# Order of the token mixers inside a two-layer decoder trunk: which attention is projected and emitted ahead of the delta rule

## The chip, the cores and the metric

One core of one Trainium2 chip. TensorE (PE) multiplies, VectorE (DVE), ScalarE (ACT) and GpSimd (POOL) do elementwise work, SyncE (SP) issues most transfers. The metric is the device time of one execution in microseconds (us), as the median of several runs; lower is better. The numbers of a profile come from one execution that was recorded.

## What is computed

A trunk of two layers over one sequence of 512 tokens with 1024 features, in float32. Each layer is a feed-forward block, a mixer and a second feed-forward block, each followed by a layer norm:

```python
x = layer_norm(ALPHA * x + 0.5 * swiglu(x, ffn1_w_gu[l], ffn1_w_down[l]), ...)
mix = hybrid_mixer(x, w_in[l], ...)
x = layer_norm(ALPHA * x + mix, ...)
x = layer_norm(ALPHA * x + 0.5 * swiglu(x, ffn2_w_gu[l], ffn2_w_down[l]), ...)
```

The mixer projects `x` by `w_in` and runs three causal mixers side by side, whose outputs are concatenated and projected by `w_out`:

- softmax (differential) attention, 4 heads: the difference of two softmaxes of 32-wide queries and keys, on 64-wide values, then an RMS norm;
- stick-breaking attention, 4 heads of 64: each score passes a log-sigmoid, a reversed running sum along the keys and an exponential, then an RMS norm;
- the gated delta rule, 4 heads of 128: queries, keys and values pass a causal convolution of width 4 and Silu; in chunks a triangular system is solved; a scan over the chunks carries a 128x128 state per head; the output is normed and multiplied by Silu of a gate projection `z`.

## The kernel before, in words

Activations lie feature by token: 8 tiles of 128 features by 512 tokens. A float32 product is three passes over a rounded part and a rest (`mm3`, L99 to L105: weight high times x high, high times low, low times high). `Stream.get` (L73 to L95) loads a chunk of 8 weight blocks, rounds four blocks on ACT (L89) and takes the rest on DVE or, where `st.eng` is set, on POOL (L90). One projection tile (`full_tile`) is 8 blocks, so 24 matmuls of 512 columns, into a PSUM bank of the pool `pd` (two in the mixer).

The program is written in an emission order, and a planner turns it into one instruction order per engine: emission order is priority, and an instruction that is ready earlier may be put ahead. On the chip each engine runs its order as it stands.

`mixer` emits for a layer, before:

1. delta projections, the first four tiles in two halves beside the norm of the feed-forward block (`first_tiles`), then the others with their convolution (`convolved`, L503 to L519: one ACT and three DVE operations) and Silu; then the ACT table of exponentials is loaded (`preload`, L478);
2. `squares` (L521), beta and decay from L549 on;
3. `project_v` (L805), 96 matmuls for the values of both attentions;
4. `triangles` (L850): key products (L537), their norms, the triangles of each head (L611 to L636), then `base` (L640), the solve of 16x16 blocks on DVE in 15 serial steps (L652, L654), reached through DRAM by transfers on SP's queue;
5. the first pair of stick-breaking query and key tiles (`project_qk`, L822). Each is split into a rounded part and a rest, and slices of the two are stacked by SBUF-to-SBUF transfers on SP (L846);
6. stick-breaking attention of heads 0, 1 and of heads 2, 3 (`attend(1, 0)` with the second pair of tiles in its middle, `attend(1, 1)`). A unit is 128 queries of one head: scores (L878, L879), ACT and DVE operations (L931 to L939), transposes (L902), a copy (L904) and the product with the values (L907). `finish` and `turned` (L970) end a pair of heads;
7. two of the four gate tiles (`gate`, L984);
8. `delta` (L859): doubling of the solved blocks (L667 to L680), joins (L686 to L705), operands (L708 to L717), and `state`, the scan over four chunks (L720 to L751), with a norm at each second chunk and a turn (L776, L779);
9. the first pair of softmax query and key tiles, softmax attention of heads 0, 1 (with the second pair in its middle) and 2, 3, with row maxima at L915;
10. the other two gate tiles, Silu of the gates (`silus`, L472, which waits behind the last exponential), product with the delta output, residual sums on POOL (L134), and `split` (L992, L993) of the eight parts;
11. the output projection by `w_out`: `head` computes four tiles first over six parts and then over the last two, in the part order 2, 3 (stick-breaking), 4 to 7 (delta), 0, 1 (softmax).

The wide tiles of queries, keys, values, convolved tiles, gates and parts come from one pool (`wide`, `KQV` = 26 buffers). Delta's work tiles `inv` have 11 buffers. `psc` (two PSUM banks) holds scores, `po` and `pt` outputs and transposes of attention; `products` borrows all four for the four heads' key products until the triangles have read them.

Of the kernel before, what the change touches and what calls it, by code (L numbers as in the profile page):

```python
# [9 lines left out]
F32 = mybir.dt.float32  # L10
# [6 lines left out]
P = 128  # L17
# [17 lines left out]
KQV = 26  # L35
# [201 lines left out]
def ffn(g, idx, final, mixes):  # L237
    nc = g.nc
    st = g.st
    with g.tc.tile_pool(name="ffn", bufs=NJ, reuse_waits="tile") as fp, \  # L240
# [8 lines left out]
        def post(j, pg, pu):  # L249
# [6 lines left out]
            if j == 4:  # L256
                g.settled = i
            nc.vector.tensor_tensor(out=sg, in0=pu, in1=sg, op=ALU.mult)  # L258
# [167 lines left out]
def mixer(g, l):  # L426
# [14 lines left out]
    def pd():  # L441
        return g.pd.tile([P, T], F32, name="pd")
# [42 lines left out]
    b0 = st.take(12 * KD)  # L485
# [3 lines left out]
    heads_in = [pd(), py(), py(), pav.tile([P, T], F32, name="po")]  # L489
    first_tiles(g, [(b0 + i * KD, p) for i, p in enumerate(heads_in)])  # L490
# [12 lines left out]
    def convolved(h, b, pre=()):  # L503
        tiles = []
        for w, dst in enumerate((kT, qT, vT)):
            if w < len(pre):
                p = pre[w]
            else:
                p = pd()
                full_tile(g, b + w * KD, p)  # L510
# [8 lines left out]
        return silus(tiles)  # L519
# [22 lines left out]

    st.eng = nc.gpsimd
    st.queue = nc.scalar
    ends = []
    for h in range(HEADS):
        ends += convolved(h, b0 + 3 * h * KD, (heads_in[:3], heads_in[3:])[h] if h < 2 else ())
    preload(ends)
    for h in range(HEADS):  # L549
        squares(h)  # L550
# [61 lines left out]
    def triangle(h):  # L612
# [10 lines left out]
        LT = mp.tile([P, NC, P], F32, name="inv", bufs=11)  # L623
# [16 lines left out]
    def base(h0, n):  # L640
# [17 lines left out]
        for h in range(h0, h0 + n):  # L658
            XT[h] = mp.tile([P, NC, P], F32, name="XT", bufs=4)
            nc.sync.dma_start(out=XT[h], in_=slabs(g.scr[1], h))  # L660
            X[h] = mp.tile([P, NC, P], F32, name="inv", bufs=11)
            nc.sync.dma_start(out=X[h], in_=slabs(g.scr[2], h))


    def double(h):
# [5 lines left out]
        Y = mp.tile([P, NC, P], F32, name="inv", bufs=11)  # L671
# [12 lines left out]
    def join(h, m):  # L684
# [6 lines left out]
        Y = mp.tile([P, NC, P], F32, name="inv", bufs=11)  # L691
# [15 lines left out]
    def operands(h):  # L707
# [3 lines left out]
        kd[h] = mp.tile([P, NC, P], F32, name="inv", bufs=11)  # L711
# [4 lines left out]
        vb[h] = mp.tile([P, NC, P], F32, name="inv", bufs=11)  # L716
# [84 lines left out]


    V = []

    def project_v():  # L805
        bv = st.take(4 * KD)
        pv = [py(), py()] + [pav.tile([P, T], F32, name=n) for n in ("po", "pt")]
        for k in range(KD):
            xhi, xlo = g.x[k]
            hi, lo = st.get(bv + 4 * k, 4)  # L810
            for c in range(NC):
                nc.tensor.matmul(out=pv[c], lhsT=xhi[:, ch(c)], rhs=hi, start=k == 0, stop=False)
                nc.tensor.matmul(out=pv[c], lhsT=xhi[:, ch(c)], rhs=lo, start=False, stop=False)
                nc.tensor.matmul(out=pv[c], lhsT=xlo[:, ch(c)], rhs=hi, start=False, stop=k == KD - 1)
        for c in range(NC):
            y = wide()
            nc.scalar.copy(out=y, in_=pv[c])
            V.append(y)

    qb, kb_, qa, ka = [], [], [], []  # L820

    def project_qk(q, k, sc, b, w):  # L822

        n = P // w
        for dst, f in ((q, sc), (k, 1.0)):
            p = pd()
            full_tile(g, b, p)
            b += KD  # L830
            hi, lo = wide(F32R), wide(F32R)
            nc.scalar.mul(out=hi, in_=p, mul=f)
            nc.vector.scalar_tensor_tensor(out=lo, in0=p, scalar=f, in1=hi.bitcast(F32), op0=ALU.mult, op1=ALU.subtract)
            if dst is q:
                rows = [[hi, lo] * (n // 2)]
            elif n == 2:
                rows = [[hi, hi], [lo, lo]]
            else:
                rows = [[hi, hi, lo, lo]]
            for i in range(n):  # L840
                own = slice(w * i, w * i + w)
                ts = []
                for r in rows:
                    t = wide(F32R)
                    for j, src in enumerate(r):
                        nc.sync.dma_start(out=t[w * j:w * j + w].bitcast(F32), in_=src[own].bitcast(F32))  # L846
                    ts.append(t)
                dst.append(ts)
# [193 lines left out]
    def head():  # L1042

        tiles = [pd(), pd(), py(), py()]
        for a, b in ((0, 6), (6, KD)):
# [7 lines left out]
            if b < KD:  # L1053
                st.use([g.ws] * 3 + [g.wx] * 5)
                for i in range(3):
                    st.get(bo + 4 * KD + i * PC)
# [194 lines left out]
```

## Time and profile before

| what | us |
|---|---|
| median of 3 runs | 2254.13 |
| lowest, highest | 2253.29, 2255.03 |
| the profiled execution | 2255.08 |
| its span, first to last instruction | 2252.1 |
| PE busy | 2141.5 |
| DVE busy | 1153.2 |
| ACT busy | 886.4 |
| POOL busy | 346.7 |

Busy time is the time in which an engine has an instruction under way; pipelined matmuls overlap, so the time from one start to the next tells what a further one costs. A wait names the instruction that ended it, as far as the semaphores tell. PEclk is the granted clock of TensorE as a share of 2.4 GHz, as a mean over a stretch.

### The profile page before, as it was taken

How to read it: one execution, taken by the hardware profiler on the slowest of the kernel's cores; microseconds unless marked ns; L12 is line 12 of the kernel's file. 1: busy time of each engine (PE TensorE's matmuls, PEld its weight loads, DVE VectorE, ACT ScalarE, POOL GpSimd, SP SyncE). 2: the span in 40 equal slices, each digit the busy share in tenths (PEclk: the TensorE clock that was granted, in tenths of full speed). 3: DMA queues.
4: the chain of work that ended last, by engine and by line, in shares of the span. 5: the costliest groups of instructions: out<-in, count | busy, mean ns of one | idle time of the engine just before them, and what ended most of it. 6: DMA issues, size and time to landing. Idle time of an engine off the chain costs nothing.

```text
span 2252.1 us, 29920 instructions
## 1 busy us (share of the span) xinstructions
PE 2141.5 (95%) x11382; PEld 1792.2 (80%) x11382; DVE 1153.2 (51%) x2347; ACT 886.4 (39%) x1755; POOL 346.7 (15%) x295
## 2 busy tenths in 40 slices
PE   8999999997988999999999999999989889999997
PEld 7888889876767888888888888898768668888886
DVE  4533436455687843333563334274566788333426
ACT  4333324545554533332443333155454635333313
POOL 1100011442113500000130000024511144000010
PEclk9999999999998999999999999999999889999998
DMA  6433323335221233332333333233442213333322
GB/s 186 128 94 97 97 75 104 94 97 135 76 67 47 84 104 100 96 94 75 113 103 96 100 94 94 66 104 103 113 101 76 76 48 103 94 95 100 96 66 94
DMA packets 89742, 213.08 MB, mean 95 GB/s; under 512 B 21840, under 2 KB 36208, under 8 KB 89600
## 3 DMA queue, kind: packets, MB, share of 16 engines
q1 hardware_dynamic: 81696, 183.27, 26.8%
q10 hardware_dynamic: 6912, 25.17, 3.7%
q0 software_dynamic: 992, 2.75, 0.7%
q8 instruction: 89, 1.46, 0.3%
q14 instruction: 53, 0.43, 0.1%
HBM read 189.64 MB, written 6.83 MB: 87 GB/s over the span
## 4 chain that ended last, share of the span: by engine, by line
PE 79%; DVE 12%; DMA 3%; ACT 2%; issue 2%; SPq 1%; POOL 1%; ACTq 0%; POOLq 0%; DVEq 0%
PE pd L104 23%; PE pd L103 23%; PE pd L105 23%; DMA wraw<-in_w 2%; DVE wlo L90 2%; PE po L907 1%; DVE x L212 1%; ACT whi L89 1%; DVE lt L166 1%; DVE at L937 1%; DMA kqv<-kqv 1%; PE psc L878 1%; DVE x L220 1%; PE pt L902 1%; DVE x L163 1%
## 5 line engine op out<-in xcount | busy, mean ns | idle before, releaser
L89 ACT CAST whi<-wraw 128x512 fp32r<-128x512 f32 x692 | 423.1, 620 | 990.8 <-PE pd L104 798.6
L90 DVE TENSOR_TENSOR wlo<-wraw,whi 128x512 fp32r<-128x512 f32 x580 | 431.0, 750 | 640.3 <-ACT whi L89 628.1
L103 PE MATMUL pd<-x,whi 128*128 128x512 f32 (+1 forms) x1888 | 714.6, 379 | 6.6 <-ACT x L1169 6.1
L104 PE MATMUL pd<-x,whi 128*128 128x512 f32 (+1 forms) x1888 | 715.6, 379 | 1.7 <-POOL x L231 1.1
L105 PE MATMUL pd<-x,wlo 128*128 128x512 f32 (+1 forms) x1888 | 713.3, 378 | 3.1 <-DVE wlo L90 3.1
L103 PEld LDWEIGHTS pd<-x,whi 128*128 128x128 f32 x1888 | 357.1, 190 | 70.9 <-ACT x L1169 6.1
L105 PEld LDWEIGHTS pd<-x,wlo 128*128 128x128 f32 x1888 | 357.6, 189 | 66.4 <-DVE wlo L90 3.3
L104 PEld LDWEIGHTS pd<-x,whi 128*128 128x128 f32 x1888 | 357.6, 189 | 66.3 <-POOL x L231 3.0
L103 PE MATMUL pd<-hhi,whi 128*128 128x512 f32 (+1 forms) x880 | 307.7, 350 | 0.0
L104 PE MATMUL pd<-hlo,whi 128*128 128x512 f32 (+1 forms) x880 | 307.6, 350 | 0.0
L105 PE MATMUL pd<-hhi,wlo 128*128 128x512 f32 (+1 forms) x880 | 307.2, 349 | 0.0
L90 POOL TENSOR_TENSOR wlo<-wraw,whi 128x512 fp32r<-128x512 f32 x112 | 151.9, 1360 | 297.8 <-ACT whi L89 214.2
L168 POOL TENSOR_TENSOR lt<-lt 128x512 f32<-128x512 f32 x26 | 39.2, 1509 | 1016.2 <-ACT lt L165 1012.1
L103 PEld LDWEIGHTS pd<-hhi,whi 128*128 128x128 f32 x880 | 165.4, 188 | 24.4
L105 PEld LDWEIGHTS pd<-hhi,wlo 128*128 128x128 f32 x880 | 165.4, 188 | 24.2
L104 PEld LDWEIGHTS pd<-hlo,whi 128*128 128x128 f32 x880 | 165.4, 188 | 24.1
L258 DVE TENSOR_TENSOR lt<-pd,lt 128x512 f32<-128x512 f32 x88 | 60.4, 690 | 112.6 <-PE pd L105 111.2
L134 POOL TENSOR_TENSOR x<-x 128x512 f32<-128x512 f32 x48 | 74.1, 1581 | 74.1 <-DVE ams L957 70.6
L515 DVE SCALAR_TENSOR_TENSOR kqv<-pd,conv,kqv 128x511 f32<-128x511 f32 (+2 forms) x54 | 40.3, 747 | 60.4 <-ACT kqv L513 59.4
L260 DVE TENSOR_TENSOR hlo<-lt,hhi 128x512 fp32r<-128x512 f32 x88 | 67.1, 765 | 6.2
L231 POOL TENSOR_TENSOR x<-x 128x256 fp32r<-128x256 f32 x60 | 45.9, 766 | 152.1 <-ACT x L229 148.3
L165 ACT ACTIVATE lt<-x 128x256 f32<-128x256 f32 (+1 forms) x58 | 29.5, 512 | 100.0 <-DVE x L163 99.8
(307 smaller groups left out, 2300.0 us busy)
## 6 DMA issues: line engine op xcount, KB each, us to landing
wraw<-in_w SPq DMA_DIRECT2D x300, 512.0 KB, 3.5
wraw<-in_w ACTq DMA_DIRECT2D x48, 512.0 KB, 3.6
kqv<-kqv SPq DMA_DIRECT2D x128, 64.0 KB, 2.0
kqv<-kqv SPq DMA_DIRECT2D x48, 128.0 KB, 3.8
scr<-zero POOLq DMA_DIRECT2D x2, 1032.0 KB, 11.4
x<-in_xT SPq DMA_DIRECT2D x8, 256.0 KB, 5.9
scr<-inv SPq DMA_DIRECT2D x8, 256.0 KB, 3.4
XT<-scr SPq DMA_DIRECT2D x8, 256.0 KB, 5.2
```

What stands on the lines that cost most here:

```text
L89: nc.scalar.copy(out=hi, in_=r)
L90: (eng or self.eng or nc.vector).tensor_tensor(out=lo, in0=r, in1=hi.bitcast(F32), op=ALU.subtract)
L103: nc.tensor.matmul(out=out, lhsT=whi, rhs=xhi, start=first, stop=False)
L104: nc.tensor.matmul(out=out, lhsT=whi, rhs=xlo, start=False, stop=False)
L105: nc.tensor.matmul(out=out, lhsT=wlo, rhs=xhi, start=False, stop=last)
L134: i = g.nc.gpsimd.tensor_tensor(out=t, in0=xhi.bitcast(F32), in1=xlo.bitcast(F32), op=ALU.add)
L165: nc.scalar.activation(out=sq[:, r], in_=t[:, r], func=AF.Square)
L168: eng.tensor_tensor(out=self.acc2[:, r], in0=self.acc2[:, r], in1=sq[:, r], op=ALU.add)
L231: eng.tensor_tensor(out=xlo[:, r], in0=t[:, r], in1=xhi[:, r].bitcast(F32), op=ALU.subtract)
L258: nc.vector.tensor_tensor(out=sg, in0=pu, in1=sg, op=ALU.mult)
L260: nc.vector.tensor_tensor(out=hlo, in0=sg, in1=hhi.bitcast(F32), op=ALU.subtract)
L515: nc.vector.scalar_tensor_tensor(out=y[:, s:], in0=p[:, :T - s], scalar=wc[:, 3 - s:4 - s], in1=y[:, s:], op0=ALU.mult, op1=ALU.add)
```

## The change

The order of emission in the mixer is turned round, and the weights are packed in the new order. The new order is: stick-breaking queries and keys (now the four tiles of `first_tiles`, stacked at once by the new helper `stack`, behind a table load that waits for the last Silu of the feed-forward block), values, beta and decay, the whole of stick-breaking attention with its `flush`; then the twelve delta projections with convolutions, Silu and a second table load, squares; then the first softmax pair, `triangles` and `delta`; then softmax attention, all four gate tiles, and the end. The last turns of the scan are set aside and put behind softmax attention. The output projection takes parts in their own order, with four attention parts first, of which all splits are on POOL; `head` is halved at four parts. `KQV` is 27 and `inv` has 10 buffers.

```diff
-KQV = 26
+KQV = 27
+            g.lastsilu = i
+    def stack(p, dst, f, w, keys):
+        n = P // w
+        hi, lo = wide(F32R), wide(F32R)
+        nc.scalar.mul(out=hi, in_=p, mul=f)
+        nc.vector.scalar_tensor_tensor(out=lo, in0=p, scalar=f, in1=hi.bitcast(F32), op0=ALU.mult, op1=ALU.subtract)
...
+                    nc.sync.dma_start(out=t[w * j:w * j + w].bitcast(F32), in_=src[own].bitcast(F32))
...
+    bq = st.take(4 * KD)
+    heads_in = [pd(), pd(), py(), pav.tile([P, T], F32, name="po")]
+    first_tiles(g, [(bq + i * KD, p) for i, p in enumerate(heads_in)])
+    st.eng = nc.gpsimd
+    st.queue = nc.scalar
+    preload([g.lastsilu])
+    for i, p in enumerate(heads_in):
+        stack(p, (qb, kb_)[i % 2], (0.125, 1.0)[i % 2], 64, i % 2)
+    project_v()
...
-        LT = mp.tile([P, NC, P], F32, name="inv", bufs=11)
+        LT = mp.tile([P, NC, P], F32, name="inv", bufs=10)
...
-    project_v()
-    triangles()
-    bq = st.take(4 * KD)
-    project_qk(qb, kb_, 0.125, bq, 64)
-    attend(1, 0, lambda: project_qk(qb, kb_, 0.125, bq + 2 * KD, 64))
-    attend(1, 1)
-    gate(2)
-    delta()
+    attend(1, 0)
+    attend(1, 1)
+    flush()
+    b0 = st.take(12 * KD)
+    tiles = []
+    for h in range(HEADS):
+        tiles += convolved(h, b0 + 3 * h * KD)
+    preload(silus(tiles))
+    for h in range(HEADS):
+        squares(h)
     bp = st.take(4 * KD)
     project_qk(qa, ka, 32.0 ** -0.5, bp, 32)
+    triangles()
+    delta()
+    turns_left = later[:]
+    del later[:]
     attend(0, 0, lambda: project_qk(qa, ka, 32.0 ** -0.5, bp + 2 * KD, 32))
-    for o in oab[2:]:
+    attend(0, 1)
+    flush()
+    for f in turns_left:
+        f()
+    gate(HEADS)
+    silus(zs)
+    for o in oab:
         split(o, nc.gpsimd)
-    attend(0, 1)
-    while later:
-        later.pop(0)()
-    gate(HEADS - 2)
-    silus(zs)
...
-    st.use([g.wx] * WX, [g.ws] * 3)
+    st.use([g.ws] * WS, [g.wx] * 2)
...
-    for o in oc + oab[:2]:
+    for o in oc:
         split(o)
-    order = [2, 3, 4, 5, 6, 7, 0, 1]
+    order = list(range(KD))
...
-        for a, b in ((0, 6), (6, KD)):
+        for a, b in ((0, 4), (4, KD)):
```

## Rows read from the trace of the kernel before

**Rows 1.** The page, part 1: busy us, share of span, instructions.
```profile
PE 2141.5 (95%) x11382; PEld 1792.2 (80%) x11382; DVE 1153.2 (51%) x2347; ACT 886.4 (39%) x1755; POOL 346.7 (15%) x295
```
**Rows 2.** Windows of layer 1's mixer: length, busy by engine, PEclk, DMA share, GB/s.
```profile
380.00:454.00 74.00, 72.51 (x417) 62.31 (x416) 38.08 (x75) 39.95 (x73) 34.13 (x31) 1.00 0.26 79
454.00:481.00 27.00, 25.49 (x112) 20.21 (x111) 8.59 (x23) 11.04 (x24) 9.84 (x8) 0.94 0.26 78
481.00:544.00 63.00, 54.93 (x311) 44.40 (x309) 47.02 (x126) 33.43 (x81) 26.75 (x22) 1.00 0.50 126
544.00:580.00 36.00, 28.83 (x184) 24.45 (x184) 18.47 (x36) 19.63 (x45) 5.42 (x3) 0.91 0.29 74
580.00:601.00 21.00, 21.00 (x257) 14.72 (x257) 6.19 (x18) 9.75 (x29) 3.84 (x3) 1.00 0.45 119
...
608.00:641.00 33.00, 32.41 (x227) 28.23 (x227) 25.69 (x97) 14.52 (x37) 0.00 (x0) 1.00 0.20 51
641.00:656.00 15.00, 13.81 (x94) 11.49 (x93) 13.16 (x56) 12.00 (x41) 4.15 (x6) 1.00 0.29 72
656.00:706.00 50.00, 35.68 (x148) 27.22 (x149) 38.19 (x95) 27.24 (x69) 10.44 (x7) 0.73 0.21 64
```
**Rows 3.** Windows of layer 2's mixer, two of its stretches.
```profile
1598.00:1660.00 62.00, 54.42 (x308) 44.07 (x307) 46.65 (x126) 32.96 (x79) 27.30 (x22) 1.00 0.52 129
...
1773.00:1823.00 50.00, 36.26 (x151) 27.56 (x150) 37.77 (x95) 27.34 (x69) 9.66 (x7) 0.73 0.20 63
```
**Rows 4.** Waits of PE, 380 to 706: total us, times, longest.
```profile
PE psc L878 <- DMA kqv<-kqv: 7.6, 3, 3.8
PE pt L970 <- DVE at L964: 6.8, 2, 4.4
```
**Rows 5.** Timeline of PE, products: start, us, tiles and shape, count.
```profile
483.76 1.06 PE L537 MATMUL pt<-kqv 128*128 128x128 f32 x8
```
**Rows 6.** Timeline of PE from 640 to 707, with idle before and its releaser.
```profile
640.22 0.39 PE L750 MATMUL pa<-vn,intra 128*128 128x128 f32 x2
...
658.44 0.39 PE L103 MATMUL pd<-kqv,whi 128*128 128x512 f32 x1
658.66 0.39 PE L104 MATMUL pd<-kqv,whi 128*128 128x512 f32 x1
...
692.06 0.73 PE L103 MATMUL pd<-kqv,whi 128*128 128x512 f32 x2 [1.80 <-ACT kqv L992]
...
704.94 0.65 PE L970 MATMUL pt<-ident,at 128*128 128x128 f32 x4 [2.33 <-DVE at L964]
```
**Rows 7.** Groups of DVE, 380 to 641: count, busy us, mean ns, idle before.
```profile
L515 DVE SCALAR_TENSOR_TENSOR kqv<-pd,conv,kqv 128x511 f32<-128x511 f32 (+2 forms) x27 | 20.2, 747 | 30.2 <-ACT kqv L513 29.7
L937 DVE TENSOR_TENSOR_SCAN at<-at 128x384 f32<-128x384 f32 (+3 forms) x16 | 15.4, 960 | 0.3
L938 DVE TENSOR_TENSOR at<-psc,at 128x384 f32<-128x384 f32 (+3 forms) x16 | 7.8, 488 | 0.3
...
L654 DVE TENSOR_TENSOR blk<-blk,blkt 128x15 f32<-128x15 f32 (+7 forms) x15 | 5.1, 342 | 0.3
```
**Rows 8.** Timeline of ACT behind the scan and at the gates' Silu.
```profile
640.64 0.37 ACT L792 COPY o<-pa 128x256 f32<-128x256 f32 x1 [0.70 <-PE pa L750]
...
649.57 0.84 ACT L779 ACTIVATE x<-pa,dng 128x256 f32<-128x256 f32 x2
...
685.86 1.28 ACT L472 ACT_TABLE_LOAD   x1
687.15 0.63 ACT L472 ACTIVATE kqv<-kqv 128x512 f32<-128x512 f32 x1
```
**Rows 9.** Groups of PE, 507 to 585: the scores of stick-breaking attention.
```profile
L878 PE MATMUL psc<-kqv 128*128 128x384 f32 (+3 forms) x32 | 10.1, 383 | 10.1 <-DMA kqv<-kqv 7.2 <-DVE at L938 1.7 <-DVE blk L654 1.2
```
**Rows 10.** Timeline of SP's queue: issues of the stacking copies.
```profile
609.09 4.94 SPq L846 DMA_DIRECT2D kqv<-kqv  x8
```
**Rows 11.** Groups of PE, 603 to 706: first passes of the output projection.
```profile
L103 PE MATMUL pd<-kqv,whi 128*128 128x512 f32 x12 | 5.6, 478 | 1.8 <-ACT kqv L992 1.8
...
L103 PE MATMUL psc<-kqv,whi 128*128 128x512 f32 x7 | 3.1, 473 | 0.0
```

More of the change, by code (lines that the diff above doesn't have):

```diff
@@ L482, in preload, with project_v, project_qk @@
             g.after(table, i)
-    b0 = st.take(12 * KD)
+    V = []
+    qb, kb_, qa, ka = [], [], [], []
+    def project_v():
+        bv = st.take(4 * KD)
+        pv = [pd(), pd()] + [pav.tile([P, T], F32, name="pt"), py()]
+        for k in range(KD):
+            xhi, xlo = g.x[k]
+            hi, lo = st.get(bv + 4 * k, 4)
+            for c in range(NC):
+                nc.tensor.matmul(out=pv[c], lhsT=xhi[:, ch(c)], rhs=hi, start=k == 0, stop=False)
+                nc.tensor.matmul(out=pv[c], lhsT=xhi[:, ch(c)], rhs=lo, start=False, stop=False)
+                nc.tensor.matmul(out=pv[c], lhsT=xlo[:, ch(c)], rhs=hi, start=False, stop=k == KD - 1)
+        for c in range(NC):
+            y = wide()
+            nc.scalar.copy(out=y, in_=pv[c])
+            V.append(y)
+    def stack(p, dst, f, w, keys):
[3 more added lines that the diff above has]
+        nc.vector.scalar_tensor_tensor(out=lo, in0=p, scalar=f, in1=hi.bitcast(F32), op0=ALU.mult, op1=ALU.subtract)
+        if not keys:
+            rows = [[hi, lo] * (n // 2)]
+        elif n == 2:
+            rows = [[hi, hi], [lo, lo]]
+        else:
+            rows = [[hi, hi, lo, lo]]
+        for i in range(n):
+            own = slice(w * i, w * i + w)
+            ts = []
+            for r in rows:
+                t = wide(F32R)
+                for j, src in enumerate(r):
+                    nc.sync.dma_start(out=t[w * j:w * j + w].bitcast(F32), in_=src[own].bitcast(F32))
+                ts.append(t)
+            dst.append(ts)
+    def project_qk(q, k, sc, b, w):
+        for keys, dst, f in ((0, q, sc), (1, k, 1.0)):
+            p = pd()
+            full_tile(g, b, p)
+            b += KD
+            stack(p, dst, f, w, keys)
+    bq = st.take(4 * KD)
[7 more added lines that the diff above has]
+    project_v()
     kT, qT, vT = [], [], []
@@ L501, in mixer, with convolved @@
     nc.scalar.copy(out=ba, in_=p[0:2 * n])
-    def convolved(h, b, pre=()):
+    def convolved(h, b):
         tiles = []
         for w, dst in enumerate((kT, qT, vT)):
[L506 to L510, printed above, removed]
+            p = pd()
+            full_tile(g, b + w * KD, p)
             y = wide()
@@ L518, in convolved @@
             tiles.append(y)
-        return silus(tiles)
+        return tiles
     def squares(h):
@@ L541, in products @@
         nc.vector.tensor_scalar(out=xs[:, 0, h], in0=xs[:, 0, h], scalar1=RMS_EPS, scalar2=None, op0=ALU.add)
[L543 to L550, printed above, removed]
     gb = pa()
@@ L670, in double @@
             nc.tensor.matmul(out=pt[:, c], lhsT=lx[:, c], rhs=X[h][:, c], start=True, stop=True)
-        Y = mp.tile([P, NC, P], F32, name="inv", bufs=11)
+        Y = mp.tile([P, NC, P], F32, name="inv", bufs=10)
         nc.scalar.copy(out=Y, in_=pt)
@@ L800, in mixer @@
     nm = Norm(g, 3 * l + 1, ALPHA, LN_EPS)
[L803 to L848, printed above, removed]
     def triangles():
@@ L1053, in head @@
             if b < KD:
+                for d in range(4):
+                    st.get(bo + d * KD + PC)
                 st.use([g.ws] * 3 + [g.wx] * 5)
-                for i in range(3):
-                    st.get(bo + 4 * KD + i * PC)
     def ahead(*pools):
@@ L1207, in split_in @@
     v = np.concatenate([va, vb], axis=1).reshape(KD, P, 4, P).transpose(0, 2, 1, 3)
-    return sum(heads, []) + [v] + pairs(qb, kb) + [blocks(z)[:2]] + pairs(qa, ka) + [blocks(z)[2:]]
+    return pairs(qb, kb) + [v] + sum(heads, []) + pairs(qa, ka) + [blocks(z)]
 def kernel(**inputs):
```

13 lines of the change are left out of this document (7 added, 6 removed).

## The prediction

> **What bounds the kernel now.** I read the page first, then the mixer's two stretches by windows, then TensorE's waits, then single lines. PE is busy 95% of the span, so a reordering can win only where it is not [rows 1]. That is the mixer. Each layer's, from its first projection to the point where the output projection runs without a break, is the stretch from 380 to 706 (326 us) in layer 1 and from 1498 to 1823 (325 us) in layer 2; the two have the same shape [rows 2, 3]. Its stages, in layer 1: delta projections 380 to 454, value projection to 481, then the delta chain 481 to 641 (products and base solve to 544, doubling to 580, joins to 601, operands to 608, scan to 641), and a tail to 706. PE idles 8.1 us in the base-solve stretch, 7.2 in the doubling stretch and 14.3 in the last 50 us, where the granted clock is a mean 0.73 as well [rows 2]; layer 2's last stretch says the same, 13.7 and 0.73 [rows 3].
>
> Two waits make up much of that. Scores of the stick-breaking attention wait for copies of stacked queries and keys (7.6 us in three waits), and the transposes of finished attention blocks wait for VectorE (6.8 us) [rows 4]. The tail has a plain cause. The gates' Silu must come behind the softmax attention's last Exp: its table load stands at 685.86 and the first Silu at 687.15 [rows 8]; the output projection of a delta head waits for its split and starts at 692.06, and the softmax attention's last transposes come at 704.94, although the scan's last matmul starts at 640.22 [rows 6]. So 65 us pass behind the scan.
>
> **The change part by part.** The kernel's instructions are ordered by a planner: emission order is priority, and a ready instruction of lower priority fills a gap. I therefore add up, per layer, a front, the delta chain and a tail.
>
> *Front.* One projection tile is 24 matmuls. At 0.23 us each (starts 658.44 and 658.66 [rows 6]) that is 5.5 us. Before, 12 delta tiles and the value projection (96 matmuls, four tiles) stand ahead of the chain: 16 x 5.5 = 88.3 us. With 16 small beta/gate matmuls (3.7 us at the same pace) and 16 transposes of the squares (at 0.11 us each, from eight that end after 1.06 us, one alone taking some 0.27 [rows 5]; 1.8 us) that is 93.8; the stretch took 101 [rows 2], so 7.2 us were lost. After, four stick-breaking tiles come ahead too: 20 x 5.5 = 110.4, plus 5.5 as before, plus the whole of stick-breaking attention, which is emitted ahead of the delta projections. Its PE work: 40 transposes and 80 value matmuls at 0.11 us (13 us), 32 score matmuls (10.1 us as pipelined busy time for the bulk of them [rows 9], about 7 by starts) and the masks: 21 us, an estimate. The sum is 137; with the loss of before, and 4 us more for friction, 148. The friction is bounded: the DVE work in this stretch is 16 scans of 0.96 us and two elementwise operations of 0.49 us beside each (31 us in all), and 36 convolution steps of 0.75 us (27 us) [rows 7]; 58 us in some 85 us of PE work is not a bound, but a convolution tile holds one of two PSUM banks for an ACT operation and three such steps, behind attention's. Between nothing and 15 us I take 4, since the stretch from 380 to 454 ran the same convolutions at 98% PE busy. Then the first pair of softmax query/key tiles, emitted ahead of the products: 11 us. It hides the last convolution, its Silu and the table load (1.28 us [rows 8]; there are two more loads per layer, one hidden here, one behind the FFN's last Silu under the projections). The chain starts at 148 + 11 = 159 us instead of 101.
>
> *Chain.* Before it is 160 us [rows 2]. What shortens it: stick-breaking attention was emitted ahead of the doubling and so had priority in it; softmax attention is emitted behind the scan and fills only. Base stretch, 63 us: the 15 steps' larger operation needs 5.1 us of DVE [rows 7], but softmax units take DVE and ACT in the same place, and products to triangles is DVE work that stays; I take 59. The copies of stacked queries and keys pass the base solve's transfers on SP's queue: the first softmax pair has 32 of them, 20 us of issue at 8 in 4.94 us [rows 10], over before the gather some 28 us into the chain. Doubling, 36 us: 7.2 idle go with the score waits, of which the longest stands inside it, and stick-breaking's own 7 us or so of PE go; 22, between 36 and the 9 us that its 80 matmuls of 128 columns need. Joins, 21 us, filled with three large matmuls in every gap: 18. Operands, the 7 us from 601 to 608, stay. Scan, 33 us, filled with softmax units in both kernels, with fewer projections after: 28. The sum is 134. Ends: 160 if nothing gets shorter; 115 if the idle 15 us and a third of the foreign PE work go (PE is busy 144 of the 160 us, some 50 of it the chain's own by counts and 0.11 us).
>
> *What fills the chain.* Softmax attention (21 to 24 us of PE), its second projection pair (11) and four gate tiles (22) are PE work of 55 us beside some 50 of the chain's own in 134. Slots decide when: 27 wide tiles hold 12 convolved, 4 value and 8 softmax tiles, so the second pair cannot be stacked before the first two softmax heads are done (about 60 us into the chain at the 4 us per unit that the tail of before shows), and comes to its end at about 120. That is ahead of the scan's end.
>
> *Tail.* Behind the last scan step of before, copy, square, norm, transposes and scaling run from 640.64 to 650.4 [rows 8]; the product with the gate and the split add 3 us. The first half of the output projection (4 tiles x 4 parts x 3 matmuls, 11 us) needs only attention outputs and hides most of it. By 706, before had issued 19 groups of three of the output projection [rows 11], against 16 here: 9 matmuls, 2 us. The tail is 15 us instead of 65. The residual sums (POOL, eight) and the attention splits move to POOL ahead of it, under the scan and the gates; uncovered, the splits would cost 6 us. Smaller pools (10 instead of 11 delta buffers) cost nothing while two buffers stay free in the doubling.
>
> *Sum.* 159 + 134 + 15 = 308 against 326: 18 us per layer, 36 in both. The profiled execution took 2255.1 us (2252.1 span and 3.0 around it), 1 us above the median: 2255.1 - 36 - 1 = **2218**.
>
> **A rule that speaks against it.** In the last 50 us of before PE is busy 35.7 us and the granted clock is a mean 0.73, between full (2.4 GHz) and half (1.2 GHz) [rows 2]; the clock fell behind PE's gaps there. The Trainium skill, "TensorE: Matmul & The Clock Gate", section "HAM oscillation — how this bites in real kernels", says that a kernel whose PE keeps pausing is throttled again and restarts cold each time. By that rule the chain, now with 55 us of filler for 134 us, would itself run cold; the trace agrees for the old tail.
>
> **The rivals.** (1) *The chain is the bound and does not shrink.* It starts 58 us later, and if it takes 160 us the mixer is 159 + 160 + 15 = 334 us, 8 more per layer: 2270, slower. It decides from a chain of 152 us on. For it: the base stretch is latency of small DVE steps and DMA round trips, and its length is the same in both layers [rows 2, 3]. Against: the waits of [rows 4] in it.
> (2) *Cold clock.* The chain's matmuls of 128 columns, 264 by the code, take 0.11 us more each at half clock, 29 us, of which I put 12 on the path, the rest beside other work: 24 us in two layers, 2242. For it: 0.91 already in the doubling stretch [rows 2]. Against: the chain is mostly DVE, ACT and DMA latency.
> (3) *Softmax attention is late.* If its second half ends 17 us behind where I put it, because slots come late, the gates' Silu waits for it as before and the mixer takes 325 us: 2252, no change that can be told.
> (4) *The chain runs nearly alone*, 115 us: 289 per layer, 2181.
> (5) *Attention and delta projections do not overlap*: attention's units are a string of ACT and DVE operations, and if the planner leaves PE idle beside them, its 16 units take some 45 us (31 of DVE alone [rows 7]) where I counted 21: 24 us per layer, 2266.
>
> **How the numbers follow.** Forecast 0.45, (1) 0.13, (2) 0.15, (3) 0.10, (4) 0.12, (5) 0.05. A change under 0.2% (4.5 us) is about what a measurement here can tell from none. Faster: forecast, (2) and (4), 0.72. (3) splits into 0.06 same and 0.04 slower; slower is 0.22. The range 2184 to 2268 leaves out half of (4) and most of (1).
>
> **What would show it.** Right: PE over 90% busy from the mixer's start to about 148 us in, with softmax scores standing between the doubling's matmuls and the gates' table load ahead of the last scan step; the stretch from the last scan matmul to unbroken output projection under 20 us. The front is wrong if PE shows gaps under the convolutions; the chain if products-to-scan-end is over 152 us; the tail if the gates' Silu still comes 20 us behind the scan. A chain under half clock over most of its length would make (2) right.

## The result, and the profile after

The changed kernel takes 2273.93 us (median of four, 2271.83 to 2275.83) beside 2253.71 us of the kernel before on the same chip: a ratio of 1.0088, 95% interval 1.0072 to 1.0103. It is 0.9% slower, where 2218 us was forecast and 2268 was the upper end of the range. Its profiled span is 2269.8 us, 17.7 more than before.

The page's first part shows that TensorE's work is the same as in [rows 1]; only the span is longer.

```profile
PE 2144.6 (94%) x11382; PEld 1789.4 (79%) x11382; DVE 1161.0 (51%) x2339; ACT 889.4 (39%) x1757; POOL 347.7 (15%) x303
```

To compare the mixers I use one mark in all kernels: the start of the 96th matmul of the output projection (as many as its first four tiles have, 4 x 8 x 3). A row of windows has the stretch, its length, the busy time of each engine with instruction counts, the granted clock (PEclk, 1 is 2.4 GHz, 0.5 is 1.2 GHz), the DMA share and GB/s. First layer 1 of the kernel before, from its first projection to that mark:

```profile
379.60:716.00 336.40, 302.05 (x1834) 247.39 (x1834) 206.12 (x541) 174.25 (x404) 95.84 (x79) 0.94 0.31 83
```

Layer 1 of the changed kernel to the same mark, by stages (front; products to the middle of the doubling; on to the scan's end; tail):

```profile
379.90:542.00 162.10, 153.38 (x849) 125.89 (x848) 88.17 (x179) 94.57 (x200) 60.83 (x50) 1.00 0.31 89
542.00:614.00 72.00, 58.03 (x317) 48.15 (x317) 46.44 (x146) 27.94 (x74) 19.62 (x17) 0.81 0.53 134
614.00:676.40 62.40, 57.16 (x521) 45.84 (x520) 41.92 (x129) 28.50 (x72) 5.09 (x5) 1.00 0.18 55
676.40:724.40 48.00, 34.58 (x153) 25.82 (x153) 35.56 (x89) 24.26 (x60) 16.02 (x15) 0.82 0.16 55
...
sum 344.50, PE 303.15 PEld 245.69 DVE 212.09 ACT 175.27 POOL 101.55; mean PE 75.79 PEld 61.42 DVE 53.02 ACT 43.82 POOL 25.39
```

TensorE is busy 302 us in the one and 303 in the other; its idle time is 34.4 us before (336.4 - 302.05) and 41.4 after (344.5 - 303.15). Of the 8.1 us of layer 1, 7.0 are idle time. Layer 2 grows by 13.2 us to the same mark (334.4 to 347.6 us), 9.3 of them idle time. Of these 21.3 us the rest of the kernel gives back 3.6.

The stages say where. The front ends at 162.4 us behind the mixer's start (forecast 159). The chain from the products' first matmul to the scan's last takes 134.1 us (forecast 134; before 159.6). From there to the mark it takes 48.0 us; before it was 75.4, and the forecast needed about 25 (before's 336.4 for layer 1, less the 18 us forecast, is 318.4; less 159 and 134). So front and chain came near the forecast (3.4 us late at the front's end in layer 1, 5.7 in layer 2), and most of the miss lies behind the scan: 23 of 26 us in layer 1 and 24 of 31 in layer 2.

**What is late there.** The timeline of ScalarE around the scan (start, us, line and operation, tiles, count, idle before). Line numbers are the changed kernel's, 3 below those of before in the attention (L904 is the product with the values, L967 and L970 are the transposes and the scaling in `turned`, L943 copies a finished half out of `po`).

```profile
626.62 0.58 ACT L943 COPY at<-po 128x512 f32<-128x512 f32 x1
...
659.84 0.37 ACT L837 COPY o<-pa 128x256 f32<-128x256 f32 x1 [2.83 <-PE pa L795]
...
669.95 0.69 ACT L970 ACTIVATE x<-pt,dfg 128x512 f32<-128x512 f32 x1
...
684.88 1.28 ACT L473 ACT_TABLE_LOAD   x1
686.17 0.63 ACT L473 ACTIVATE kqv<-kqv 128x512 f32<-128x512 f32 x1
```

And TensorE in the same stretch and in the tail:

```profile
649.86 0.49 PE L967 MATMUL pt<-ident,at 128*128 128x128 f32 x3
...
671.18 0.49 PE L899 MATMUL pt<-ident,at 128*128 128x128 f32 x3
...
687.92 0.43 PE L904 MATMUL po<-kqv,at 128*128 128x64 f32 x2 [0.35 <-ACT at L901]
695.94 1.09 PE L967 MATMUL pt<-ident,at 128*128 128x128 f32 x4 [7.58 <-DVE at L961]
698.91 1.22 PE L103 MATMUL pd<-kqv,whi 128*128 128x512 f32 x2 [1.89 <-ACT kqv L989]
```

The first half of softmax attention is copied out at 626.62, but its scaling stands at 669.95, 43 us later. In between lie its norm, 16 VectorE operations, most of 0.16 us, drawn out from 630.60 to 648.91 between those of the joins and the scan, and 20 us in which the finished transposes stand in the one bank `pt` while ScalarE has gaps of some 3 us. No transposes of a unit (L899) start between 620 and 671: the closing transposes stand ahead of them in `pt`. No row maximum (L912) starts between 638.5 and 677. So the second half does not run in the scan; its last product is at 687.92, 12 us behind the scan's last matmul (676.38). Behind its last exponential (683.76) come the gates' table load and Silu as before [rows 8]; behind its last product come the closing norm (TensorE idles 7.58 us for it) and the split. The output projection of a tile begins with the softmax parts, so ahead of the split only the 12 matmuls of the first half's part run (674.99 to 685.60).

### The profile page after: what moved, and what is told of

Read it like the earlier page. It is cut to its first block, busy times and chain, and to the rows that moved or that the text cites. A ratio compares the mean times of both kernels' runs of the same rounds, so it can differ in the third digit from the quotient of the medians.

```text
span 2269.8 us, 29990 instructions
## 1 busy us (share of the span) xinstructions
PE 2144.6 (94%) x11382; PEld 1789.4 (79%) x11382; DVE 1161.0 (51%) x2339; ACT 889.4 (39%) x1757; POOL 347.7 (15%) x303
## 4 chain that ended last, share of the span: by engine, by line
PE 74%; DVE 13%; DMA 5%; ACT 4%; issue 2%; POOL 1%; SPq 1%; ACTq 0%; POOLq 0%; DVEq 0%
PE pd L104 22%; PE pd L103 22%; PE pd L105 22%; DMA wraw<-in_w 5%; DVE wlo L90 2%; PE po L904 1%; ACT whi L89 1%; DVE x L212 1%; PE psc L875 1%; DVE x L220 1%; POOL wlo L90 1%; DVE x L163 1%; DVE lt L166 1%; DVE x L162 0%; DVE kqv L569 0%
## 5 line engine op out<-in xcount | busy, mean ns | idle before, releaser
L103 PE MATMUL pd<-x,whi 128*128 128x512 f32 (+1 forms) x1920 | 725.2, 379 | 11.5 <-ACT x L1177 6.3
L105 PE MATMUL pd<-x,wlo 128*128 128x512 f32 (+1 forms) x1920 | 724.3, 378 | 2.7 <-DVE wlo L90 2.7
L104 PE MATMUL pd<-x,whi 128*128 128x512 f32 (+1 forms) x1920 | 724.5, 378 | 1.6 <-POOL x L231 1.2
L103 PEld LDWEIGHTS pd<-x,whi 128*128 128x128 f32 x1920 | 363.7, 190 | 77.2 <-ACT x L1177 6.3
L105 PEld LDWEIGHTS pd<-x,wlo 128*128 128x128 f32 x1920 | 364.3, 190 | 66.1 <-DVE wlo L90 2.9
L104 PEld LDWEIGHTS pd<-x,whi 128*128 128x128 f32 x1920 | 364.1, 190 | 65.7 <-POOL x L231 3.0
L103 PE MATMUL pd<-hhi,whi 128*128 128x512 f32 (+1 forms) x880 | 307.8, 350 | 0.0
L569 DVE SCALAR_TENSOR_TENSOR kqv<-pd,conv,kqv 128x511 f32<-128x511 f32 (+2 forms) x72 | 53.4, 742 | 35.9 <-ACT kqv L567 34.9
L231 POOL TENSOR_TENSOR x<-x 128x256 fp32r<-128x256 f32 x60 | 45.1, 753 | 160.8 <-ACT x L229 157.4
## 6 DMA issues: line engine op xcount, KB each, us to landing
scr<-zero POOLq DMA_DIRECT2D x2, 1032.0 KB, 11.3
```

The lines of the kernel that those rows point to most:

```text
L103: nc.tensor.matmul(out=out, lhsT=whi, rhs=xhi, start=first, stop=False)
L104: nc.tensor.matmul(out=out, lhsT=whi, rhs=xlo, start=False, stop=False)
L105: nc.tensor.matmul(out=out, lhsT=wlo, rhs=xhi, start=False, stop=last)
L231: eng.tensor_tensor(out=xlo[:, r], in0=t[:, r], in1=xhi[:, r].bitcast(F32), op=ALU.subtract)
L569: nc.vector.scalar_tensor_tensor(out=y[:, s:], in0=p[:, :T - s], scalar=wc[:, 3 - s:4 - s], in1=y[:, s:], op0=ALU.mult, op1=ALU.add)
```

## Experiments

The theory: the second half of softmax attention misses the scan, and the output projection waits for it. Rivals: the order of the output projection's parts alone costs the time; the base solve, bared of large matmuls, costs it; or the work is only work. All times below stand beside runs of the kernel before on the same chip (medians 2253 to 2256), so a difference of some 2 us between two kernels can be the chips'. Chain, attention and mark are of layer 1 and counted from the mixer's start, worked out from the timelines' starts and ends; busy and idle are TensorE's over a window that ends within 0.4 us of the mark.

| kernel | us | ratio to before, 95% | products to scan's end | last softmax product | mark | busy | idle |
|---|---|---|---|---|---|---|---|
| before | 2253.7 | | 159.6 | 310.6 | 336.4 | 302.1 | 34.4 |
| after | 2273.9 | 1.0088 (1.0072 to 1.0103) | 134.1 | 308.5 | 344.5 | 303.2 | 41.4 |
| t1_order | 2273.6 | 1.0095 (1.0079 to 1.0110) | 134.9 | 307.8 | 344.8 | 304.9 | 40.0 |
| t2_pd | 2306.5 | 1.0239 (1.0216 to 1.0262) | 145.0 | 294.0 | 367.4 | 322.4 | 45.1 |
| t3_first | 2250.4 | 0.9985 (0.9976 to 0.9995) | 144.1 | 281.7 | 331.9 | 301.7 | 30.2 |
| t7_qk | 2260.7 | 1.0030 (1.0017 to 1.0042) | 140.9 | 303.6 | 340.1 | 302.4 | 38.0 |
| t4_half | 2231.6 | one run | 131.2 | (left out) | 321.9 | 291.9 | 30.2 |
| b1_stick_behind | 2276.6 | 1.0107 (1.0088 to 1.0127) | 144.8 | 322.6 | 349.9 | 309.5 | 40.8 |
| t8_first_qk | 2249.1 | 0.9972 (0.9954 to 0.9991) | 145.5 | 278.8 | 325.9 | 295.2 | 30.9 |
| t10_first_qk_gate | 2247.4 | 0.9977 (0.9965 to 0.9989) | 145.7 | 295.6 | 333.6 | 298.3 | 35.1 |
| t11_order2 | 2268.8 | 1.0071 (1.0044 to 1.0097) | 138.6 | 313.0 | 341.7 | 303.3 | 38.4 |
| t12_gate_order2 | 2251.2 | 0.9985 (0.9973 to 0.9998) | 152.2 | 302.3 | 333.0 | 299.3 | 33.7 |
| t13_qk_order2 | 2252.7 | 0.9996 (0.9977 to 1.0014) | 158.6 | 290.0 | 338.3 | 305.7 | 32.6 |
| t14_first_qk_gate1 | 2262.9 | 1.0024 (1.0012 to 1.0036) | 153.8 | 298.7 | 341.3 | 304.7 | 36.6 |

### The lateness priced: without the second half

```diff
-    attend(0, 1)
     flush()
+    oab[1] = oab[0]
```

> The changed kernel without the second half of the softmax attention: its units, its second projection pair still made, and its output replaced by the first half's; 10 to 12 us of TensorE work per layer is left out. It prices the lateness of that half. Theory (the tail waits for the softmax attention): the 96th matmul of the output projection comes more than 20 us sooner per layer, that is, by more than the work left out; the stretch from the scan's end to it falls from 48 us to under 30, near the forecast's 26: 2225 to 2235. Rival (work is only work): it falls by the 10 to 12 us left out: 2250.

Measured: 2231.6 us, in a single run. Layer 1 comes to the mark some 22 us sooner (344.5 to 321.9; the rows below end 0.3 us behind it). The first row below is the whole stretch, the second the tail from the scan's end.

```profile
379.40:701.50 322.10, 291.87 (x1740) 235.53 (x1739) 192.63 (x481) 159.52 (x359) 96.10 (x83) 0.96 0.34 91
...
673.40:701.50 28.10, 25.21 (x99) 19.51 (x100) 22.99 (x53) 11.34 (x26) 5.91 (x7) 0.88 0.23 68
```

Of the 22.4 us between the two rows of the whole stretch (344.5 to 322.1), 11.3 are TensorE work left out (303.15 to 291.87) and 11.1 are idle time that went with it. The tail is 28.1 us against a forecast of some 25. The forecast's tail exists, but only when softmax attention is out of the way. Half of what the second half costs here is TensorE's waiting, not its work.

### Priority: the first half ahead of the doubling

```diff
+    attend(0, 0, lambda: project_qk(qa, ka, ...))
+    flush()
     delta()
     turns_left = later[:]
     del later[:]
-    attend(0, 0, lambda: project_qk(qa, ka, ...))
     attend(0, 1)
```

> The changed kernel with the first half of the softmax attention, its closing transposes too, emitted ahead of the doubling instead of behind the scan, so with priority over it. Theory (priority): the first half's norm, drawn out from 631 to 649 us behind the joins' VectorE work, is done before the joins end, and the second half runs in the scan: the tail falls by 10 us or more per layer, the chain grows by less than 5: about 2262. Rival (the chain pays): the units go back to where stick-breaking attention stood in the kernel before, the chain grows from 134 towards 150 us and takes the gain back: 2270 to 2290.

Measured: 2250.4 us, 23.5 below the changed kernel and 0.15% below the kernel before. ScalarE's timeline now has the first half's copy and scaling 7 us apart instead of 43, and the gates' table load ahead of the scan's last matmul (687.67 + 0.39 us):

```profile
596.15 0.59 ACT L943 COPY at<-po 128x512 f32<-128x512 f32 x1 [0.78 <-PE po L904]
...
602.93 0.69 ACT L970 ACTIVATE x<-pt,dfg 128x512 f32<-128x512 f32 x1 [5.53 <-PE pt L967]
...
655.39 1.28 ACT L473 ACT_TABLE_LOAD   x1
```

```profile
379.60:543.00 163.40, 155.51 (x845) 127.48 (x845) 87.98 (x179) 94.51 (x199) 60.71 (x50) 0.98 0.30 87
543.00:623.00 80.00, 66.98 (x363) 55.62 (x363) 52.52 (x167) 33.90 (x87) 19.82 (x18) 0.81 0.52 132
623.00:689.00 66.00, 59.70 (x544) 49.45 (x543) 49.15 (x144) 34.59 (x92) 11.94 (x14) 0.97 0.13 41
689.00:711.50 22.50, 19.51 (x86) 15.03 (x87) 18.68 (x47) 9.66 (x23) 3.72 (x3) 1.00 0.15 50
```

The last softmax product comes 26.8 us sooner (308.5 to 281.7), and the tail falls from 48.0 to 22.5 us with 3.0 us idle instead of 13.4. The chain pays 10 us for it (144.1), twice what the theory allowed, and the gain was twice as large as well. Both the theory and its rival name something real. No run here with all the work in it has a chain of 134 us and a short tail at once. The chain of 131.2 us with a tail of 28.1 came only where the second half was left out: part of what makes the chain short is that attention does not run in it.

### The one bank

```diff
     def turned(which, j, o):
-        pt = pav.tile([P, T], F32, name="pt")
+        pt = pav.tile([P, T], F32, name="pt") if which else pd()
```

> The changed kernel with one PSUM bank exchanged: the transposes that close a half of the softmax attention take a projection's bank (pd) in place of the one bank (pt) that the units' own transposes need. Theory (held bank): in the changed kernel the first half's closing transposes stand in pt from 650 to 670 us, because ScalarE's scaling out of it comes late in its order, so that no unit of the second half runs in the scan. With another bank the second half runs under the joins and the scan, its last row maximum ahead of the scan's end (some 297 us behind the mixer's start), and the stretch from the last scan matmul to the 96th of the output projection falls from 48 us to about 33: 10 to 15 us per layer, 2244 to 2254. Rival (the chain fills up): the units take TensorE, ScalarE and VectorE from the scan, which then ends later by what the tail gains: 2268 to 2276.

Measured: 2306.5 us. The held bank did keep the second half back: transposes of its units now run from 636.62 to 654.69, ahead of the closing ones at 656.85, though the scaling still stands at 681.97. Its last product comes at 294.0 instead of 308.5, but these 14.5 us are not the bank's alone, since `pd` is the bank of the gate tiles too, which move behind the closing transposes and leave the chain to the attention. Their copies on ScalarE, all ahead of 653 us in the changed kernel, now stand at 694 to 712:

```profile
693.66 0.58 ACT L981 COPY kqv<-pd 128x512 f32<-128x512 f32 x1
694.26 1.28 ACT L473 ACT_TABLE_LOAD   x1
...
712.02 0.58 ACT L981 COPY kqv<-pd 128x512 f32<-128x512 f32 x1
712.81 0.63 ACT L473 ACTIVATE kqv<-kqv 128x512 f32<-128x512 f32 x1
```

So 22 us of large matmuls left the chain for the tail. Neither theory had that. Of the 19 us more busy time, none is more work; the granted clock over the whole stretch is 0.88 where it was 0.94.

### The order of the output projection, twice

```diff
-    for o in oab:
+    for o in oab[2:]:
         split(o, nc.gpsimd)
...
-    st.use([g.ws] * WS, [g.wx] * 2)
+    st.use([g.wx] * WX, [g.ws] * 3)
-    for o in oc:
+    for o in oc + oab[:2]:
         split(o)
-    order = list(range(KD))
+    order = [2, 3, 4, 5, 6, 7, 0, 1]
-        for a, b in ((0, 4), (4, KD)):
+        for a, b in ((0, 6), (6, KD)):
...
```

> The changed kernel with the kernel before's order of the output projection: the splits of stick-breaking attention stand ahead, then the delta heads', the softmax parts last, and the first pass takes six parts instead of four. Theory (order): the changed kernel loses behind the scan because the first pass of the output projection begins with the two softmax parts, which are the last to be ready; six other parts, 72 matmuls of 0.23 us (17 us), can run while the softmax attention ends. The 96th matmul of the output projection then comes 8 to 10 us sooner per layer: about 2256 us, within 3 us of the kernel before. Rival (lateness alone): the delta heads' parts are just as late, since their gates' Silu stands behind the last Exp in both orders; less than 3 us per layer comes back: 2268 to 2274.

Measured: 2273.6 us, no change. It is not a clean price: with this order the first weights go to the pool that opens only when attention's work tiles close, so they come late: from 641 to 678 us the DMA queues move nothing (0 GB/s), where the changed kernel's move 45 GB/s from 640 to 676. TensorE's longest waits from 678 to 726 us are these:

```profile
PE pd L103 <- ACT whi L89: 6.5, 2, 4.2
PE pd L105 <- DVE wlo L90: 4.4, 1, 4.4
```

So the order was tried again with the changed kernel's pools and passes:

```diff
-    for o in oab:
+    for o in oab[2:] + oab[:2]:
         split(o, nc.gpsimd)
...
-    order = list(range(KD))
+    order = [2, 3, 0, 1, 4, 5, 6, 7]
```

> The changed kernel with one exchange: within the first four parts of the output projection the stick-breaking parts come first, then the two softmax parts; their splits likewise. Pools and passes are the changed kernel's. Each of the four banks of the first pass sums its parts in that order, so in the changed kernel the second part, the late one, holds up the two behind it. Theory (order, in the form that the earlier run on order did not price, since there the delta heads came ahead of the softmax parts): 24 matmuls more can run ahead of the last softmax part, 3 to 6 us per layer, 2262 to 2268. Rival (no bank: two of the four banks hold scores until the last units, and TensorE at half clock eats the rest): 2270 to 2275.

Measured: 2268.8 us, 5.1 below the changed kernel, just outside what the theory expected; the four times lie from 2264 to 2277 and the two intervals overlap. The 24 matmuls do run ahead: in layer 1, 36 of the output projection have started by 692.83 instead of 12. But the last softmax product comes 4.5 us later, and the mark only 2.8 us sooner (7.1 in layer 2). So the order is worth some 3 to 7 of the 23 us missing per layer, and the lateness remains.

### The base solve and the first softmax pair

```diff
-    project_qk(qa, ka, 32.0 ** -0.5, bp, 32)
     triangles()
+    project_qk(qa, ka, 32.0 ** -0.5, bp, 32)
```

> The changed kernel with the first pair of softmax query and key tiles emitted behind the products, the norms, the triangles and the base solve instead of ahead of them. Theory (bare base solve): the changed kernel has put all large matmuls ahead of the chain, so TensorE stands still for 8 us at the end of the base solve and the doubling begins at a granted clock of 0.83; with 48 matmuls (11 us) left for it, the chain starts 11 us sooner, TensorE works in the base solve, and 8 to 11 us per layer come back: 2252 to 2258. Rival (the tail sets the end): the softmax attention starts later by what the chain gains, and the output projection waits for it as before: 2268 to 2276.

Measured: 2260.7 us, 13.2 below the changed kernel, between what the theory and its rival expected. The products start at 150.7 us instead of 162.4, and TensorE's wait of 7.6 us for the solved blocks at the end of the base solve is gone, but another has taken its place. This is the largest from 531 to 600 us:

```profile
PE psc L875 <- DMA kqv<-kqv: 6.8, 2, 4.6
```

It is for the stacking copies, which are issued from SP's queue, as the base solve's transfers are. The stretch still idles: 13.4 of 58.0 us, at a mean granted clock of 0.85. The gain comes from the chain's earlier start, not from a filled base solve; of the 11.7 us by which the chain starts sooner in layer 1, its greater length takes back 6.8.

```profile
531.00:589.00 58.00, 44.61 (x228) 35.40 (x226) 42.11 (x127) 23.28 (x54) 23.19 (x20) 0.85 0.51 128
```

### The chain's term, tested on the kernel before

```diff
-    attend(1, 1)
     gate(2)
     delta()
+    attend(1, 1)
```

> The kernel before with the second half of stick-breaking attention emitted behind the delta chain instead of ahead of the doubling. Theory (the forecast's term for the chain: attention with priority over the chain lengthens it): products to the scan's end falls from 160 us to about 150, and the attention that is moved comes out at the tail, so that the time hardly changes: 2250 to 2270. Rival (the chain is latency of small steps and of transfers, as the first rival of the prediction has it): the chain stays within 3 us of 160, and the time rises by what the tail gets, 2265 to 2280.

Measured: the chain falls from 159.6 to 144.8 us, and the time rises by 23 us, beyond the theory's 2270. It is the same trade as the change's: attention behind the chain shortens the chain by 15 us and comes out at the tail, dearer than it was. TensorE's rows at the two ends of the chain (products' first matmuls, scan's last):

```profile
480.98 1.95 PE L537 MATMUL psc<-kqv 128*128 128x128 f32 x16
...
625.40 0.39 PE L750 MATMUL pa<-vn,intra 128*128 128x128 f32 x2
```

### Both gains together, and gates for the base solve

The edits of t3_first and t7_qk together:

> Both edits that gave time back, together: the first half of the softmax attention emitted ahead of the doubling, and the first pair of softmax query and key tiles behind the base solve. Theory (two places: the softmax attention ends too late, and the chain starts 11 us later than it need): the gains of 23.5 and 13.2 us add up, 2237 us, and a layer's idle time of TensorE to the 96th matmul of the output projection falls from 41 to about 24 us. Rival (one gain twice: each edit only lets the second softmax half into the scan): 2248 to 2252.

Measured: 2249.1 us, the rival's number; but the twelve single times lie near 2239 (four), 2250 (seven) and 2260 (one). Layers 1 and 2 of the profiled execution (2248.5 us) suggest why. Both to the mark:

```profile
379.90:706.00 326.10, 295.19 (x1835) 240.69 (x1834) 212.49 (x539) 172.28 (x401) 97.78 (x84) 0.95 0.32 89
1487.70:1825.30 337.60, 306.46 (x1836) 248.69 (x1835) 212.25 (x538) 171.79 (x400) 97.78 (x84) 0.92 0.31 86
```

and their joins, behind the doubling, from first matmul to last; layer 2's also in two pieces:

```profile
612.20:631.90 19.70, 19.48 (x253) 13.46 (x252) 9.80 (x27) 12.80 (x36) 0.00 (x0) 1.00 0.24 72
1720.90:1750.10 29.20, 28.98 (x253) 19.60 (x252) 9.91 (x26) 12.75 (x36) 0.00 (x0) 0.61 0.20 62
...
1720.90:1727.10 6.20, 5.98 (x101) 4.01 (x99) 2.18 (x8) 3.73 (x12) 0.00 (x0) 1.00 0.59 187
1727.10:1750.10 23.00, 23.00 (x158) 15.59 (x153) 7.73 (x19) 9.01 (x25) 0.00 (x0) 0.50 0.09 28
```

Idle time is the same, 30.9 and 31.1 us; busy time differs by 11.3 us, and 9.5 of it are the joins: at full clock in layer 1, and from 1727.1 on at half in layer 2. Two layers like the first would give the times near 2239, where the two gains add up (the theory's 2237). No execution near 2239 was profiled, so this is not shown; it fits that the mean granted clock of the whole execution goes with the groups: 0.978 to 0.980 near 2239, 0.973 to 0.976 near 2250, and 0.970 at 2260. But the theory's other sign did not come: idle time is 31 us, where it expected 24.

Then two of the four gate tiles ahead of softmax attention, as filler for the base solve:

```diff
     project_qk(qa, ka, 32.0 ** -0.5, bp, 32)
+    gate(2)
     attend(0, 0, ...)
...
-    gate(HEADS)
+    gate(HEADS - 2)
```

> The run with both edits, and two of the four gate tiles (48 matmuls, 11 us) emitted ahead of the softmax attention, so with priority over it. Theory (nothing large is left for the end of the base solve, where TensorE stands still for 13 us): the tiles stand there, and up to 8 us per layer come back, 2222 to 2235. Rival (slots: the wide tiles are all held, so that the gates cannot start there, or the weights for them arrive late): within 4 us of the run without this edit. Second rival: the gate tiles hold wide tiles that the second softmax pair needs, and it is stacked later: 3 to 10 us slower than the run without the edit.

Measured: 2247.4 us, far from the theory's 2222 to 2235 and within 4 us of the run without the edit, and the two layers alike: 333.6 and 333.4 us to the mark. The gates stand in the base solve, and the doubling starts 5 us later for it. Softmax attention ends 17 us later than without this edit (295.6 against 278.8), which is the second rival's direction. What it brings is evenness (its ten runs lie from 2245.6 to 2251.2), not time.

> The run with both edits and the two early gate tiles, and with the stick-breaking parts first in the output projection. In the run without this exchange the second softmax half ends at the scan's end, 295 us behind the mixer's start, its split at 310, and only 12 matmuls of the output projection run ahead of it, while TensorE idles 12 us in the last 38 and the granted clock there is 0.82. Theory (the late part holds up the ones behind it): 24 matmuls more in that stretch, 5 to 8 us per layer, 2231 to 2238. Rival (the delta heads' last splits come as late, and they end the stretch whatever is ahead): 2243 to 2248.

With the stick-breaking parts first as well: 2251.2 us, above both expectations. Here too 24 matmuls more run ahead of the late part (36 instead of 12), yet the mark hardly moves (333.0); the chain is 6.5 us longer.

> The run with both edits but no early gate tiles, and with the stick-breaking parts first in the output projection. There the softmax attention is done ahead of the delta heads, so the order among the first four parts should matter little. Theory: 2244 to 2249, and the single times still fall in groups some 10 us apart, as they did (2238 to 2240, 2249, 2260), each group by whether the joins of a layer run at full or at half granted clock. Rival: the order gives 5 us per layer here too, 2239.

Both edits with that part order and no early gates: 2252.7 us, above both expectations, with single times from 2239 to 2266. In the profiled execution (2265.4 us) the joins take 29.2 and 29.0 us in the two layers, as in layer 2 above.

```diff
-    gate(2)
+    gate(1)
-    gate(HEADS - 2)
+    gate(HEADS - 1)
```

> The run with both edits, and one of the four gate tiles (24 matmuls, 5.5 us) ahead of the softmax attention instead of none or two. Theory (one tile stands in the base solve's last third, where TensorE idles and the granted clock is 0.67, and takes no wide tile that the second softmax pair needs): the joins run at full clock in both layers, as with two tiles, and the softmax attention ends ahead of the scan, as with none: the 96th matmul of the output projection at about 326 to 329 us behind the mixer's start in both layers, 2236 to 2243. Rival (the tile only puts the doubling off, and whether the joins run cold is set by other things): 2246 to 2252.

One gate tile instead of two, in the kernel t10_first_qk_gate: 2262.9 us, worse than none and than two, and than either expectation. The chain takes 153.8 us. Why one tile is worse than either is not settled; the planner's order differs in many places.

The two lowest, both edits with and without two early gate tiles, cannot be told apart (2247.4 and 2249.1 us, ratios 0.9977 and 0.9972). They are 0.2 to 0.3% below the kernel before and some 1.1% below the changed kernel.

## Why the prediction was wrong, step by step

*Front.* Near: 159 forecast, 162.4 and 164.7 measured in the two layers, with TensorE 95% busy (153.4 of 162.1 us). Stick-breaking attention and the delta projections do overlap, so rival (5) is out.

*Chain.* The length came out, 134.1 and 135.0 against 134, but to the microsecond it is luck: its parts miss by 2 or 3 us with both signs (products to doubling 57 where 59 was forecast, doubling 19 for 22, joins 21 for 18, scan 30 for 28), and the second half of softmax attention, which I had put into it, was mostly not there. With more attention in it the chain takes 144.1 us (t3_first). The cause that I gave holds: taking half of stick-breaking attention out of the chain of before shortens that to 144.8 us. Rivals (1) and (4) are out. One row that I used is another layer's: the score waits of 7.6 us in [rows 4] are of layer 2; from 380 to 706 they are 7.2 us.

*What fills the chain.* Here it fails. I let the second half of softmax attention end some 120 us into the chain; it ended at 146 (308.5 - 162.4), behind the scan. The gates' table load, which I expected ahead of the last scan step, came 8.5 us behind it (684.88). The reason I gave for caution, slots for the second pair, was not the one: the second pair was stacked 43 to 72 us into the chain, as I had said. What I left out is that work emitted behind the chain has its small VectorE and ScalarE steps behind the chain's as well, and that the step which closes a half holds the bank that the next half needs. I had counted filler as TensorE microseconds (55 into 134) and not as a string of dependent steps on three engines. The exchange of the bank, with the gates out of the way, brought 14.5 us of that lateness back, the priority 26.8. Why the planner put the scaling as late as 669.95 isn't shown.

*Tail.* The mis-sized term: 15 us forecast to the unbroken output projection, and 27.5 measured (scan's end at 676.4, TensorE without a pause from 703.88). At that point 19 matmuls of the output projection had been issued, where before had issued 54 at 706 (I took 57 from the groups of [rows 11]): 35 matmuls at 0.23 us, 8 us more, of which I had counted 2. The other 77 up to the mark took 20.5 us instead of 17.7, the first of them at half clock. I had hidden 11 us of the output projection, 48 matmuls, under the scan's closing norm because it "needs only attention outputs". These were the last to come, and 12 of the 48 ran early. Without the second half the stretch from the scan's end to the mark is 28.1 us, and with priority for the first half 22.5, near the 25 that the forecast needed.

*The rivals.* (3) is what happened, though not for its reason (slots): the second half ended 26 us behind where I had put it. I priced it at 2252 with a chance of 0.10, because I took the mixer to come out at its old length. It comes out longer, since the front had grown by 61 us and chain and tail gave back 25.5 and 27.4. (2), the cold clock, did not decide here: joins and scan ran at 1.00. The stretch with the base solve was at 0.81 and the tail at 0.82; over the mixer it is 0.94, as before.

*A test that would have told.* The forecast of 318.4 us to the mark in layer 1 leaves 16 us of idle time beside TensorE's 302, which the change does not alter. Before had 34. For the 18 us that would have to go I had 7 in the doubling and the tail's 14, and I set nothing against them for what a base solve without large matmuls loses. After, that was 13.3 us in the base solve's stretch alone (5.7 + 7.6; the stretch to 614 has 14.0). No kernel here came below 30.

## What to carry to other kernels

When an engine is over 90% busy and a change only reorders its work, check a sum of stages against that engine's work plus its idle time: what idle time does the forecast leave, and who fills it? Filler behind a latency chain is not free to fill: its own short steps on the other engines queue behind the chain's, and a single buffer at its closing step can stop it for the length of a stage. Emit just the part of the filler ahead of the chain that must end early; here one half of it turned 0.9% slower into 0.15% faster.

## What the runs showed of the hardware

In the run with both edits, the same TensorE instructions in the same order (joins of layers 1 and 2), behind a doubling that ran at full clock in both layers, ran at a granted clock of 1.00 in one layer and 0.61 in the other, in one execution. In layer 2 the clock fell to its half level at 1727.1, with TensorE busy 10.9 of the 11.1 us before and all of the 23 us behind. That cost 9.5 us of busy time in the joins. The times of that kernel lie in groups some 10 us apart, which would be one such layer more or less; this is argued from two profiled executions (one layer in 2248.5 us; two in 2265.4 us, with another order of parts). What decides it is open. In both layers the stretch ahead of the doubling was alike, 26 us with some 14.3 us busy at 0.67. The rule that I had weighed, in the Trainium skill, "TensorE: Matmul & The Clock Gate", section "HAM oscillation — how this bites in real kernels" (an engine that keeps pausing restarts cold each time), agrees with the 0.67 there; it does not tell the two layers' joins apart, in which TensorE was busy 99% of the time.
